# Splitting the expert combine of an MoE layer into two F32R passes with one-hot rows, and moving the token gather between two transposes

## The chip, the cores and the metric

One core of a Trainium2 chip (trn2) runs the whole program. The metric is the device time of one execution in microseconds (us). Timings of such a program differ a little from run to run, so times are medians of several runs, and changes are judged beside runs of the unchanged kernel.

## What is computed

One layer of a hybrid encoder on 256 tokens of 1024 features, all float32: a mixer (differential attention on half of the channels, a gated linear recurrence on the other half), a LayerNorm, then a mixture of experts (top 4 of 32), and a last LayerNorm. Only the mixture is touched here. Cut to what matters:

```python
def clamped_swiglu(h):
    x_glu = jnp.minimum(h[..., ::2], 7.0)
    x_lin = jnp.clip(h[..., 1::2], -7.0, 7.0)
    return x_glu * jax.nn.sigmoid(1.702 * x_glu) * (x_lin + 1.0)

def moe(x, w_router, b_router, w_gu, b_gu, w_down, b_down):
    logits = xt @ w_router + b_router
    top_v, top_e = lax.top_k(logits, 4)
    gates = jax.nn.softmax(top_v, axis=-1)
    ...
    def expert_block(args):
        tok, g, e = args
        xb = xt[tok]
        h = xb @ w_gu[e] + b_gu[e]
        y = clamped_swiglu(h) @ w_down[e] + b_down[e]
        return y * g[:, None].astype(y.dtype)
    ...
    out = jax.ops.segment_sum(ys.reshape(R, D), row_tok, num_segments=T)
```

Each expert has 12 MB of float32 weights (8 MB in `w_gu`, 4 MB in `w_down`), so that the 32 experts read some 403 MB from HBM.

## The kernel before

After the mixer and the router, the program walks over the 32 experts (`for e in range(NE - 1)`, line 1090, and a tail for the last one from line 1126). Each expert has 64 slots (CAP) for its tokens; slots beyond that are computed in an overflow path behind a branch (`overflow`, `more`), which this input takes once. The work of expert e, in the order in which TensorE (PE) does it:

1. `first(e)`: the up projection (`gu_mm`, L892), 64 matmuls into the PSUM tiles h0 and h1. The four 2 MB chunks of `w_gu` are used one after the other. Behind each half VectorE (DVE) and ScalarE (ACT) compute the clamped SwiGLU (`swiglu`, L902 to L906); for the second half this begins when the last matmul is through.
2. `finish(e % 2)`: the combine (L954) of the pair of experts before: the output rows of two experts lie on 128 partitions, and a matmul with the transposed gate matrix `gt` (slots by tokens, the gate's value where slot and token meet, else 0) spreads them over the tokens. DVE adds the result to `acc` (L956). One half of the tokens is combined in the even expert behind the pair, the other half in the odd one.
3. In an even expert GpSimd (POOL) builds the gate rows `sgate` for the pair (`gate_rows`, L940). In an odd one PE transposes them (`gate_t`, L948) and ACT copies them out of PSUM as `gt` (L950).
4. For each half b: two transposes of the activations (`act_t`, L913) into PSUM, ACT copies them out (L914), and `begin_gu` starts the PSUM tile h of the next expert with its bias (L679).
5. `need(...)`: a matmul with a one-hot matrix S gathers one half of the next pair's token rows (`gather_mm`, L797); ACT (even) or DVE (odd) copies them out (L807, L805). POOL makes S (L784).
6. The down projection (`down_mm`, L925), 32 matmuls into the tiles y0 and y1, and, after an odd expert, ACT copies both to SBUF (L1117) for the combine.

Steps 2 to 5 stand between the up and the down projection of one expert. The transposes, the gather, the combine and the copied gates all take their PSUM tiles from one pool of three buffers (`mc`), so that each of them waits until the reader of an earlier tile is done. The order on PE and on the DMA queue (SP) is the program's; on DVE, ACT and POOL a scheduler sets it when the program is built, except in the tail, where DVE and ACT are ordered by hand.

The weights come over SP's queue in the order of use (`load_chunk`), into ten buffers of 2 MB (`SLOTS`): each load waits until PE is through with the chunk that lay in its buffer.

In the tail, expert 31 and the last LayerNorm: four PSUM tiles `fps` collect `acc` and the last combines (`fin`, L1130). Two of these matmuls are strewn between the down projection of expert 30 (`todo`), and four follow the last down projection, after ACT and DVE have copied y0 and y1 (L1166, L1167).

## Time and profile before

| | |
|---|---|
| median of 3 runs | 1098.46 us (1097.53 to 1099.27) |
| the profiled execution | 1100.57 us, its span 1098.9 us |
| granted TensorE clock, mean | 0.979 of full speed |
| PE busy | 1008.3 us (92%) |
| DVE, ACT, POOL busy | 277.8, 188.7, 146.6 us |
| read from HBM | 420.52 MB, 384 GB/s over the span |

The span is what lies between the first and the last instruction that the profiler saw; the execution's time has some 1.7 us more around it. [...] The durations of matmuls are those of one instruction from start to end; since they are pipelined, the distance from start to start is what they cost.

### The profile page before, as it was taken

The page shows a single profiled execution, that of the slowest core. Times are in us where ns is not written, and L with a number is a line of the kernel's source. Part 1 is how long each engine was busy: PE and PEld are TensorE (multiplying, and loading weights), DVE is VectorE, ACT ScalarE, POOL GpSimd, SP SyncE. Part 2 cuts the span into 40 slices and gives each one's busy share as a digit, 9 for nine tenths or more (in the row PEclk, how much of TensorE's full clock was granted, in tenths as well). Part 3 has the DMA queues.
Part 4 walks back from the last instruction along what each step waited for, and adds up shares of the span by engine and source line. Part 5 has one row for each costly group of instructions (what it writes and reads, how often), then busy time and mean ns, then how long its engine had stood idle before and what let it go on. Part 6 is the DMA issues. An engine that isn't in the chain of part 4 may idle for free. (4 is left out here: it accounts for less than half of the span.)

```text
span 1098.9 us, 12603 instructions
## 1 busy us (share of the span) xinstructions
PE 1008.3 (92%) x4948; PEld 472.8 (43%) x4948; DVE 277.8 (25%) x625; ACT 188.7 (17%) x426; POOL 146.6 (13%) x221
## 2 busy tenths in 40 slices
PE   8999999999999889888999989888888989999995
PEld 8987644443444333333334433333323434444431
DVE  6978411121212121213212121212101222121223
ACT  5576211111111111110011111110100101111111
POOL 4583202010101010101001010101001001010101
PEclk8999999999999999999899999999999989999998
DMA  7967799999999999999999999999999949999972
GB/s 268 334 247 318 293 377 426 422 423 423 423 423 423 422 423 423 422 425 426 423 424 420 410 423 412 420 410 394 415 395 411 423 198 424 425 425 422 424 292 82
DMA packets 47193, 423.44 MB, mean 385 GB/s; under 512 B 6365, under 2 KB 6430, under 8 KB 14400
## 3 DMA queue, kind: packets, MB, share of 16 engines
q1 hardware_dynamic: 47040, 421.59, 92.9%
q8 instruction: 73, 1.20, 0.5%
q14 instruction: 80, 0.66, 0.2%
HBM read 420.52 MB, written 1.05 MB: 384 GB/s over the span
## 5 line engine op out<-in xcount | busy, mean ns | idle before, releaser
L892 PE MATMUL h<-we,xg 128*64 128x512 f32 (+1 forms) x2112 | 469.8, 603 | 63.1 <-DMA we<-in_w_gu_dram 50.6
L892 PEld LDWEIGHTS h<-we,xg 128*64 128x64 f32 (+1 forms) x2112 | 161.9, 137 | 368.3 <-issue 295.1
L925 PE MATMUL y<-we,actT 128*64 128x512 f32 x1024 | 228.9, 599 | 0.1
L902 DVE TENSOR_SCALAR g<-h 128x256 f32<-128x256 f32 x65 | 27.6, 425 | 688.3 <-PE h L892 688.3
L940 POOL TENSOR_SCALAR sgate<-iota,posm,gate 128x64 f32<-128x64 f32 x96 | 54.1, 582 | 814.2 <-PE gt_ps L948 813.2
L925 PEld LDWEIGHTS y<-we,actT 128*64 128x64 f32 x1024 | 71.3, 137 | 135.1 <-issue 127.7
L903 ACT ACTIVATE sg<-g 128x256 f32<-128x256 f32 x65 | 27.0, 416 | 589.2 <-DVE g L902 589.2
L797 PE MATMUL xg_ps<-S,n 128*128 128x128 f32 (+1 forms) x544 | 70.5, 284 | 0.0
L797 PEld LDWEIGHTS xg_ps<-S,n 128*128 128x128 f32 x544 | 69.5, 199 | 2.5 <-issue 1.6
L954 PE MATMUL cb<-ysb,gtT 128*128 128x512 f32 x116 | 57.5, 618 | 0.0
L1117 ACT ACTIVATE ysb<-y 128x512 f32<-128x512 f32 x30 | 16.3, 594 | 140.7 <-PE y L925 140.7
L956 DVE TENSOR_TENSOR acc<-acc,cb 128x512 f32<-128x512 f32 x58 | 39.5, 680 | 0.0
L805 DVE TENSOR_SCALAR xg<-xg_ps,gb 128x128 f32<-128x128 f32 (+1 forms) x68 | 22.8, 398 | 61.8 <-PE xg_ps L797 61.8
L389 PE MATMUL pj<-xh,hi 128*128 128x256 f32 x128 | 37.3, 292 | 0.0
L389 PE MATMUL pj<-xh,lo 128*128 128x256 f32 x128 | 36.8, 288 | 0.0
L389 PE MATMUL pj<-xo,hi 128*128 128x256 f32 x128 | 36.8, 288 | 0.0
L913 PE MATMUL actT_ps<-ident,g 128*128 128x128 f32 x130 | 29.9, 312 | 7.3 <-DVE g L906 6.3
L954 PEld LDWEIGHTS cb<-ysb,gtT 128*128 128x128 f32 x116 | 19.6, 189 | 37.4 <-ACT sg L903 23.5
L252 POOL TENSOR_TENSOR lo<-win,hi 128x1024 fp32r<-128x1024 f32 x11 | 32.9, 3014 | 12.3 <-PE pj L389 12.2
L913 PEld LDWEIGHTS actT_ps<-ident,g 128*128 128x128 f32 x130 | 21.6, 202 | 24.8 <-DVE g L906 12.2
L807 ACT ACTIVATE xg<-xg_ps,gb 128x128 f32<-128x128 f32 (+1 forms) x68 | 25.4, 452 | 33.2 <-PE xg_ps L797 33.2
L679 PE MATMUL h<-bgu,pick 128*128 128x512 f32 x64 | 30.5, 479 | 0.0
(271 smaller groups left out, 702.5 us busy)
## 6 DMA issues: line engine op xcount, KB each, us to landing
we<-in_w_gu_dram SPq DMA_DIRECT2D x128, 2048.0 KB, 15.3
we<-in_w_down_dram SPq DMA_DIRECT2D x127, 1024.0 KB, 30.4
win<-in_w_in_dram SPq DMA_DIRECT2D x8, 1024.0 KB, 9.8
wout<-in_w_out_dram SPq DMA_DIRECT2D x4, 1024.0 KB
win<-in_w_in_dram SPq DMA_DIRECT2D x4, 512.0 KB, 8.2
x<-in_x_dram SPq DMA_DIRECT2D x4, 256.0 KB, 3.1
we<-in_w_down_dram SPq DMA_DIRECT2D x2, 512.0 KB
out_dram<-acc SPq DMA_DIRECT2D x4, 256.0 KB, 2.3
```

The lines of the kernel that those rows point to most:

```text
L252: return (eng or V).tensor_sub(lo, src, f32(hi))
L389: PE.matmul(ps[m // 2][:, m % 2], a, b, start=k == 0 and m % 2 == 0 and i == 0, stop=k == KT - 1 and i == 2, skip_group_check=True)
L679: PE.matmul(ps[b], picks[e].rearrange("p g w -> p (g w)"), bgs[b], start=True, stop=False, skip_group_check=True)
L797: PE.matmul(ps[:, (k % 4) * n:(k % 4 + 1) * n], pairs(n1[t])[:, k // 2, k % 2], S[:, t], start=start, stop=t == NT - 1, skip_group_check=True)
L892: PE.matmul(ps[b][g * w:(g + 1) * w], xg[k // 4][:, k % 4, o:o + w], W[e, k][:, c0:c0 + 512], start=False, stop=k == KT - 1, skip_group_ch ...
L902: V.tensor_scalar(g[:, ns], ps[b][:, 0::2], 7.0, None, op0=OP.min)
L903: A.activation(s, g[:, ns], AF.Sigmoid, scale=1.702)
L913: PE.transpose(ps[:, j * P:(j + 1) * P], gj[:, j], ident)
L925: PE.matmul(ps[n][gs], at[:, 2 * b + j, g * CAP:(g + 1) * CAP], w_dn(e, 2 * g + b, j, n * 512, 512), start=c + j == 0, stop=c + j == 4, sk ...
L940: G.tensor_scalar(sg[:, t, i * CAP:(i + 1) * CAP], iota2[:, 0], posm[:, t, o:o + 1], gate[:, t, o:o + 1], op0=OP.is_equal, op1=OP.mult)
L954: PE.matmul(pp, gt[:, n, t * P:(t + 1) * P], y, start=True, stop=True)
L956: V.tensor_add(acc[t][:, ns], acc[t][:, ns], pp)
```

## The change

The gates leave the combine's matrix. `gate_t` still transposes the gate rows, but ACT now copies them with two instructions, one for each expert of the pair's slot block, each of which also sums its rows (`accum_out`): since a slot holds one token, the sum is the slot's gate, in a column `gs`. POOL then turns the copy `gg` into a matrix of zeros and ones (`is_gt`), typed float32r. `weighted` takes the place of the two plain copies of y: ACT writes the gated rows as a float32r high part, and DVE (`scalar_tensor_tensor`) what is left of them as a low part. The combine is then two F32R matmuls, high and low, in place of one float32 matmul, both in the loop and in `fin`. In the tail, too, ACT and DVE now write a high and a low part of both tiles. Apart from that the gather (`need`) moves from behind both halves' transposes to between them.

```diff
-    def ytile(e, n):
-        return wk.tile([P, 512], F32, tag=f"y{n}", bufs=1, name=f"ysb{e}_{n}")
+    def weighted(e, n, src, gs):
+        hi, lo = [wk.tile([P, 512], F32R, tag=f"y{i}{n}", bufs=1, name=f"y{i}_{e}_{n}") for i in range(2)]
+        A.activation(hi, src, AF.Copy, scale=gs[:, n:n + 1])
+        V.scalar_tensor_tensor(lo, src, gs[:, n:n + 1], f32(hi), op0=OP.mult, op1=OP.subtract)
+        return hi, lo
 
     def gate_rows(e):
...
                 PE.transpose(ps[:, n, t * P:(t + 1) * P], sg[:, t, n * CAP:n * CAP + P], ident)
-        gt = wk.tile([P, 2, T], F32, tag="gtT", bufs=1, name=f"gtT{e}")
-        A.activation(gt, ps, AF.Copy)
-        return gt
+        gs = wk.tile([P, 2], F32, tag="gs", name=f"gs{e}")
+        gg = wk.tile([P, 2, T], F32, tag="ggT", bufs=1, name=f"ggT{e}")
+        for n in range(2):
+            A.activation(gg[:, n], ps[:, n], AF.Identity, bias=zero_t, accum_out=gs[:, n:n + 1])
+        gt = wk.tile([P, 2, T], F32R, tag="gtT", bufs=1, name=f"gtT{e}")
+        G.tensor_scalar(gt, gg, 0.0, None, op0=OP.is_gt)
+        return gt, gs
 
     def combine(t, n, y, gt, pp):
-        PE.matmul(pp, gt[:, n, t * P:(t + 1) * P], y, start=True, stop=True)
+        for i in range(2):
+            PE.matmul(pp, gt[:, n, t * P:(t + 1) * P], y[i], start=i == 0, stop=i == 1)
...
             if e < NE - 2:
                 begin_gu(e + 1, (b,))
-        need(where[e][0] + 1, G, where[e][1])
+            if b == 0:
+                need(where[e][0] + 1, G, where[e][1])
...
         if e % 2:
-            pend = [ytile(e, n) for n in range(2)], gt
-            for n in range(2):
-                A.activation(pend[0][n], ps[n], AF.Copy)
+            pend = [weighted(e, n, ps[n], gs) for n in range(2)], gt
...
         A.activation(warm, eps_t, AF.Sqrt)
-        A.activation(y[0], ps[0], AF.Copy)
-        V.tensor_copy(y[1], ps[1])
+        y = [weighted(e, n, ps[n], gs) for n in range(2)]
         for t in range(NT):
             fin(t, gt, y, stop=True)
```

What the change moves is read from the order of the instructions as built (the line numbers of the changed kernel are up to ten higher; [waits ...] names the engines whose results an instruction waits for). First PE in expert 29, an odd one, between its up and its down projection; cb are the combine's tiles, gt_ps the transposed gates, actT_ps the transposed activations, h30 the next expert's bias, xg_ps the gather. Before:

```order
L954 MATMUL cb29_0_33999<-ysb27_0_31894,gtT27_31843 128x512 [waits DVE_49,PE_49,Activation_49]
L954 MATMUL cb29_1_34002<-ysb27_1_31895,gtT27_31843 128x512 [waits DVE_49]
L948 MATMUL gt_ps29_34005<-ident_169,sgate28_32921 128x128 x4
L913 MATMUL actT_ps29_34013<-ident_169,g29_33984 128x128 [waits DVE_49]
L679 MATMUL h30_0_34019<-bgu0_148,pick30_34017 128x512
L913 MATMUL actT_ps29_34021<-ident_169,g29_33984 128x128 [waits DVE_49]
L679 MATMUL h30_1_34025<-bgu1_149,pick30_34017 128x512 [waits PE_49]
L797 MATMUL xg_ps_34028<-S30_32943,n1_0_1213 128x128 [waits Activation_49]
```

And with the change:

```order
L964 MATMUL cb29_0_34165<-y0_27_0_32054,gtT27_32003 128x512 [waits DVE_49,PE_49,Activation_49]
L964 MATMUL cb29_0_34165<-y1_27_0_32055,gtT27_32003 128x512
L964 MATMUL cb29_1_34169<-y0_27_1_32058,gtT27_32003 128x512 [waits DVE_49]
L964 MATMUL cb29_1_34169<-y1_27_1_32059,gtT27_32003 128x512
L952 MATMUL gt_ps29_34173<-ident_169,sgate28_33087 128x128 x4
L913 MATMUL actT_ps29_34185<-ident_169,g29_34150 128x128 [waits DVE_49]
L679 MATMUL h30_0_34191<-bgu0_148,pick30_34189 128x512
L797 MATMUL xg_ps_34194<-S30_33103,n1_0_1213 128x128 [waits PE_49,Activation_49]
L913 MATMUL actT_ps29_34207<-ident_169,g29_34150 128x128 [waits DVE_49]
L679 MATMUL h30_1_34211<-bgu1_149,pick30_34189 128x512
```

The gather now stands ahead of the second half's transposes, and its PSUM tile is the one that gt_ps held: it waits for ACT to have read the gates out. Next ACT in the same expert, before:

```order
L903 ACTIVATE sg29_33986<-g29_33984 128x256
L903 ACTIVATE sg29_33993<-g29_33984 128x256
L950 ACTIVATE gtT29_34010<-gt_ps29_34005 128x512
L914 ACTIVATE actT29_34012<-actT_ps29_34013 128x256
L914 ACTIVATE actT29_34012<-actT_ps29_34021 128x256
```

And with the change:

```order
L903 ACTIVATE sg29_34152<-g29_34150 128x256
L903 ACTIVATE sg29_34159<-g29_34150 128x256
L957 ACTIVATE ggT29_34179,gs29_34178<-gt_ps29_34173,zero_t_177 128x256 x2
L914 ACTIVATE actT29_34184<-actT_ps29_34185 128x256
L914 ACTIVATE actT29_34184<-actT_ps29_34207 128x256
```

One copy has become two that also sum, at the same place. Last DVE between the two projections of expert 28, from the second half's SwiGLU on, before:

```order
L902 TENSOR_SCALAR g28_32900<-h28_1_31858 128x256 [waits PE_49]
L904 TENSOR_SCALAR l28_32908<-h28_1_31858 128x256
L905 SCALAR_TENSOR_TENSOR l28_32908<-l28_32908,g28_32900 128x256 [waits DVE_49]
L956 TENSOR_TENSOR acc0_78<-acc0_78,cb28_0_32915 128x512 [waits PE_49]
L906 TENSOR_TENSOR g28_32900<-l28_32908,sg28_32909 128x256 [waits DVE_49,Activation_49]
L956 TENSOR_TENSOR acc0_78<-acc0_78,cb28_1_32918 128x512 [waits PE_49]
```

And with the change:

```order
L902 TENSOR_SCALAR g28_33064<-h28_1_32032 128x256 [waits PE_49]
L904 TENSOR_SCALAR l28_33072<-h28_1_32032 128x256
L966 TENSOR_TENSOR acc0_78<-acc0_78,cb28_0_33079 128x512 [waits PE_49]
L905 SCALAR_TENSOR_TENSOR l28_33072<-l28_33072,g28_33064 128x256 [waits DVE_49]
L966 TENSOR_TENSOR acc0_78<-acc0_78,cb28_1_33083 128x512 [waits PE_49]
L906 TENSOR_TENSOR g28_33064<-l28_33072,sg28_33073 128x256 [waits DVE_49,Activation_49]
```

Both additions to acc now stand ahead of the last step of the SwiGLU (L906), where one stood before. The odd experts and expert 30 have the same order. SP's queue holds the same loads in the same order.

## Rows read from the trace of the kernel before

**Rows 1.** Waits between engines, whole span: who waited, us in all, times, longest.

```profile
PE h L892 <- DMA we<-in_w_gu_dram: 50.6, 39, 2.4
```

**Rows 2.** Windows: length, busy us of PE, PEld, DVE, ACT, POOL (instructions), clock, DMA share, GB/s.

```profile
720.00:760.00 40.00, 32.79 (x152) 12.45 (x154) 4.95 (x12) 3.44 (x10) 0.00 (x0) 1.00 0.98 398
...
896.00:900.00 4.00, 3.56 (x11) 0.99 (x10) 0.76 (x2) 0.00 (x0) 0.00 (x0) 0.59 0.08 29
...
1062.00:1064.00 2.00, 2.00 (x12) 0.61 (x10) 1.82 (x5) 0.42 (x1) 0.00 (x0) 1.00 0.42 172
```

**Rows 3.** Timeline of PE, 850 to 1099 us: start, length, instruction, idle before it.

```profile
879.85 3.50 PE L892 MATMUL h<-we,xg 128*32 128x512 f32 x16 [2.40 <-DMA we<-in_w_gu_dram]
...
896.83 15.58 PE L892 MATMUL h<-we,xg 128*64 128x512 f32 x64 [0.45 <-PEq L1017]
```

**Rows 4.** SP's own waits, 860 to 930 us.

```profile
SPq L199 <- PE h L892: 25.9, 3, 19.9
```

**Rows 5.** PE by line, 897 to 1085 us: busy us, mean ns, idle before.

```profile
L892 PE MATMUL h<-we,xg 128*64 128x512 f32 x448 | 99.7, 602 | 1.3 <-PEq L1011 0.9 <-PEq L1017 0.4
```

**Rows 6.** Timeline, 962 to 980 us: expert 27 (odd) between its projections.

```profile
964.94 1.98 PE L954 MATMUL cb<-ysb,gtT 128*128 128x512 f32 x4
...
965.39 0.41 DVE L904 TENSOR_SCALAR l<-h 128x256 f32<-128x256 f32 x1
...
966.18 0.68 DVE L956 TENSOR_TENSOR acc<-acc,cb 128x512 f32<-128x512 f32 x1
...
966.76 0.60 PE L948 MATMUL gt_ps<-ident,sgate 128*128 128x128 f32 x4
...
966.77 0.42 DVE L906 TENSOR_TENSOR g<-l,sg 128x256 f32<-128x256 f32 x1
...
967.39 0.60 ACT L950 ACTIVATE gtT<-gt_ps 128x512 f32<-128x512 f32 x1 [1.42 <-PE gt_ps L948]
...
968.42 2.04 PE L797 MATMUL xg_ps<-S,n 128*128 128x128 f32 x16
...
970.39 7.09 PE L925 MATMUL y<-we,actT 128*64 128x512 f32 x32
```

**Rows 7.** Timeline, 988 to 1000 us: expert 28 (even).

```profile
991.55 1.98 PE L954 MATMUL cb<-ysb,gtT 128*128 128x512 f32 x4
...
996.40 4.08 PE L925 MATMUL y<-we,actT 128*64 128x512 f32 x18
```

**Rows 8.** Timeline of PE, 84 to 128 us: F32R matmuls of 512 columns behind float32 transposes.

```profile
113.49 0.48 PE L653 MATMUL mix<-hio,rech 128*128 128x512 f32 x1
113.81 0.40 PE L653 MATMUL mix<-hio,reco 128*128 128x512 f32 x1
114.05 0.40 PE L653 MATMUL mix<-loo,rech 128*128 128x512 f32 x1
```

**Rows 9.** Timeline of ACT, 53 to 62 us: copies of 256 columns that also sum.

```profile
56.06 0.49 ACT L453 ACTIVATE s<-s,mx 128x256 f32<-128x256 f32 x1
...
56.55 0.49 ACT L453 ACTIVATE s<-s,mx 128x256 f32<-128x256 f32 x1
56.95 0.19 ACT L453 ACTIVATION_READ_ACCUMULATOR s<-s,mx 128x1 f32 x1
```

**Rows 10.** Timeline, 1040 to 1099 us: experts 30 and 31 and the tail.

```profile
1045.97 0.42 DVE L906 TENSOR_TENSOR g<-l,sg 128x256 f32<-128x256 f32 x1
...
1066.32 0.60 PE L948 MATMUL gt_ps<-ident,sgate 128*128 128x128 f32 x4
...
1067.63 0.51 PE L913 MATMUL actT_ps<-ident,g 128*128 128x128 f32 x2 [0.47 <-ACT actT L914]
...
1072.85 1.12 PE L1130 MATMUL fin<-ysb,gtT 128*128 128x512 f32 x2
...
1084.14 0.60 ACT L1166 ACTIVATE ysb<-y 128x512 f32<-128x512 f32 x1 [6.60 <-PE y L925]
...
1088.53 0.70 DVE L1173 BATCH_NORM_STATS2 st<-fin 128x6 f32<-128x512 f32 x1
```

## The prediction

> **What bounds the kernel now.** First the waits between engines: PE waited 39 times for weights at the up projection, 50.6 us in all, so that the weights' transfers set the pace somewhere [rows 1]. Then windows, to see where. From 160 us to 880 us the transfers are at work all the time; from 720 us to 760 us, for one, with a share of 0.98, while PE is busy for only 32.79 of 40 us [rows 2]. There a faster PE only waits longer. Then PE's timeline around the one overflow, in front of expert 25. PE still waits 2.40 us for weights in it, at 879.85 us [rows 3]; whatever PE won or lost before is forgotten there. While the overflow runs, all ten buffers fill up, and SP waits 19.9 us for PE to free the next one [rows 4]: the transfers are then half an expert behind, but PE has ten chunks in hand. Expert 25 begins at 896.83 us [rows 3], and from there to the last down projection the up projections idle for 1.3 us in all, none of it for weights [rows 5]. The transfers are at work all that time too, but PE is behind them: their share falls in the window that begins at 1062 us, when the last chunk lands [rows 2], and PE needs that chunk in the second half of the down projection that ends at 1084.14 us [rows 10], in the last 3.5 us or so. That leaves PE a good 15 us to win before the weights could bind again.

> So the change counts for what it does to PE from 896.83 us on, in experts 25 to 31, and in the tail. The 23 combines before that are worth nothing, and what the changed gates cost there costs nothing, because the wait at 879.85 us takes both up.

> **The combine itself.** The four instructions of one expert's combine take 1.82 us to the next instruction's start (964.94 to 966.76 us [rows 6]). Four F32R matmuls of the same shape: behind float32 work the first takes 0.32 us to the next start, the following ones 0.24 us [rows 8], so about 1.02 us. PE saves 0.80 us per expert, if nothing else is late.

> [...]

> **Even experts (26, 28).** The first half's transposes follow at 1.02 us, the bias at about 1.17 us, the gather at about 1.5 us: it needs the tile of the first combine, which DVE has read by then (below). The gather takes 1.97 us to the next start [rows 6], and now covers the second half's SwiGLU, which ends at about 2.75 us. With 0.5 us for the second transposes and bias the down projection begins at 4.0 us. It began at 4.85 us (991.55 to 996.40 us [rows 7]). Saving: 0.85 us each, 1.7 us for both.

> **DVE's new order.** In expert 27 the second half's L904 begins 0.45 us behind the combine's start, an addition takes 0.59 us to the next start, and the last step, L906, begins at 1.83 us [rows 6]. Now the first addition begins at 0.80 us (L904 takes 0.35 us) and ends near 1.48 us; L905, with 0.34 us, and the second addition, with 0.59 us, follow, and L906 begins at about 2.32 us, 0.49 us later than before, and ends at 2.75 us. Where the gather stands in between this is hidden. Its cover is gone in expert 30, which has no gather: there the second half's transposes wait for L906, which ran at 1045.97 us [rows 10] and comes 0.49 us later. Cost: 0.5 us, once.

> **Odd experts (25, 27, 29).** The transposed gates now begin at 1.02 us, and ACT can read them 0.63 us later (966.76 to 967.39 us [rows 6]), at 1.65 us. It now runs two copies of 256 columns that sum. Such copies start 0.49 us apart, and the read of the sum ends 0.59 us behind the second's start [rows 9]: 1.08 us, or 2.7 us on this clock. The gather needs this very tile and waits for the second sum, some 1.2 us behind its place in the line; it began at 3.48 us and now at about 2.75 us. Then 1.97 us of gather and 0.5 us of transposes and bias: the down projection begins at 5.2 us. It began at 5.45 us [rows 6]. Saving: 0.2 us each, 0.6 us for three. Those copies read SBUF and also take an exponential; the nearest other row is the plain copy of 512 columns out of PSUM, 0.60 us [rows 6]. If the two sums together take no longer than that, 0.7 us are saved; if each takes as long, nothing is. These are the bounds; I stay with the row that sums.

> **Expert 31 and the tail.** The two sums stand in front of the activations on ACT here as well. They could begin at 1066.95 us and end at 1068.0 us, and the second transposes, which ran at 1067.63 us [rows 10], now wait for them: 0.4 us lost (0 to 0.9 us; the upper end is both sums and one more copy). The two combines strewn between the down projections take 1.06 us each (1072.85 us to the next down matmul); as F32R 0.32 + 0.24 us and the same 0.1 us of changeover: 0.4 us saved each, 0.8 us. Behind the last down projection ACT writes the first high part in 0.60 us from 1084.14 us, DVE the low part in 0.7 us behind it, then the second; the last matmuls are no longer four slow ones in a row. DVE, with two low parts and four statistics to do one behind the other, is the limit: its last statistics ran at 1088.53 us [rows 10] and come at about 1088.3 us. I take 0.2 us; the bounds are 0.5 us lost, if each high part holds up its low part and the matmul behind it, and 0.5 us saved.

> **Costs put at nothing.** DVE's low parts and POOL's `is_gt` run behind the down projections, 14 us or more ahead of the combine that reads them; POOL is busy for 146.6 of 1098.9 us. On POOL the next S stands behind `is_gt`, and the gather that reads it comes 20 us later. No load moves on SP. The low parts free y0 and y1 about a microsecond later; the next pair needs these some 20 us later.

> **The sum**: 1.7 + 0.6 - 0.5 - 0.4 + 0.8 + 0.2 = 2.4 us saved. Against the profiled execution's 1100.57 us that is 1098.2 us; that execution is 2.1 us above the median of the runs, and the span's proportions hold for both, so against 1098.46 us I predict **1096.1 us**. With all bounds at their worst the saving is about 0.6 us, at their best 4.6 us: 1093.9 to 1097.9 us.

> **Rivals.**
> - *The new waits don't bind.* If ACT's sums and DVE's additions are ahead of PE, each of the six combines saves its 0.80 us, or 0.85 us, and the tail 1.0 us: 5.9 us, 1092.6 us. For it: the gather as a cover is long. Against it: its PSUM tile is the gates' own, and the row for ACT's start leaves little doubt.
> - *The waits eat the saving.* If each sum on ACT takes 0.2 us longer than the row says and the tail's splits cost 0.5 us, the odd experts lose 0.2 us each and some 0.5 us remain: 1098.0 us, no change. For it: two engines, ACT and DVE, now work in series where each had one copy.
> - *The clock falls* (the slower side). In each odd expert PE now stands still for about 1.2 us in front of the gather, behind low work. If the granted clock falls on that, the next up projection pays: behind the overflow, with 0.59 granted in its first 4 us [rows 2], one took 15.58 us [rows 3], where the others average 14.0 us ((99.7 - 15.58) / 384 x 64 [rows 5]). Three times 1.6 us are 4.8 us, less 2.4 us: 1100.9 us. It decides if the clock falls in two of the three. Against it: from 720 to 760 us PE stood still for 7.2 us in pieces and the granted clock was 1.00 [rows 2]. [...]

> **How the numbers follow.** The sum 0.68, waits not binding 0.10, waits eating the saving 0.17, the clock 0.05. A measurement of this kernel can tell about 0.2% from no change, 2.2 us, and the sum lies just beyond that: 0.43 of its 0.68 go to faster and 0.25 to the same. Faster is 0.43 + 0.10 = 0.53, slower 0.05 and 0.01 from the second rival, the same 0.25 + 0.16 = 0.41. The range takes the sum's bounds, most of the second rival, and 0.7 us above it for the spread of the runs; it leaves the first rival and the third out: 1093.8 to 1098.6 us.

> **What would show it.** In the profile after: combines of four F32R instructions in about 1.0 us; even experts with 4.0 us and odd ones with 5.2 us from combine to down projection; in odd ones the gather waiting for ACT; the wait at about 879.85 us and the start of expert 25 where they were; no wait for weights behind it. It would be wrong if expert 25 began elsewhere by more than a microsecond, or if PE waited for weights again behind it.

## The result, and the profile after

The changed kernel takes 1105.17 us (median of 5 runs, 1103.85 to 1105.42), the kernel before 1098.46 us beside it (5 runs): a ratio of 1.0055, 95% interval 1.0040 to 1.0069. By that ratio it is slower by 6.0 us (4.4 to 7.6 us), and the prediction had it faster. The profiled execution of the changed kernel is its median run, with a span of 1103.4 us, 4.5 us more than before's, whose profiled execution was 2.1 us above its median.

The steps that the prediction named did what it said, nearly. An odd expert between its projections, in the timeline of the changed kernel (start, length, engine and line, instruction, idle before):

```profile
970.35 1.20 PE L964 MATMUL cb<-y,gtT 128*128 128x512 f32 x4
...
971.39 0.60 PE L952 MATMUL gt_ps<-ident,sgate 128*128 128x128 f32 x4
...
972.09 0.47 ACT L957 ACTIVATE ggT<-gt_ps,zero_t 128x256 f32<-128x256 f32 x1 [0.69 <-PE gt_ps L952]
...
972.66 0.42 DVE L906 TENSOR_TENSOR g<-l,sg 128x256 f32<-128x256 f32 x1
972.91 0.20 ACT L957 ACTIVATION_READ_ACCUMULATOR ggT<-gt_ps,zero_t 128x1 f32 x1
...
973.16 2.15 PE L797 MATMUL xg_ps<-S,n 128*128 128x128 f32 x16 [0.56 <-ACT ggT L957]
...
975.70 4.51 PE L925 MATMUL y<-we,actT 128*64 128x512 f32 x20
```

The four F32R matmuls take 1.04 us to the next start, where the old combine, two float32 matmuls that the profile shows as four instructions, took 1.82 us [rows 6]. ACT's two sums take 1.02 us (972.09 to 973.11 us), the gather waits for the second, and the down projection begins 5.35 us behind the combine; it was 5.45 us [rows 6]. An even expert, from the same view:

```profile
996.86 1.20 PE L964 MATMUL cb<-y,gtT 128*128 128x512 f32 x4
997.89 0.39 PE L913 MATMUL actT_ps<-ident,g 128*128 128x128 f32 x2
...
998.46 1.77 PE L797 MATMUL xg_ps<-S,n 128*128 128x128 f32 x13
```

Its down projection begins at 1000.98 us, 4.12 us behind the combine; it was 4.85 us [rows 7].

What nobody had asked for stands in the waits between engines from 897 us on (who waited for what: us in all, times, longest):

```profile
PE h L892 <- issue: 3.1, 1, 3.1
PE xg_ps L797 <- ACT ggT L957: 1.6, 3, 0.6
PE actT_ps L913 <- DVE g L906: 1.4, 1, 1.4
PE actT_ps L913 <- ACT ggT L957: 0.9, 1, 0.9
PE fin L1143 <- ACT y L934: 0.9, 1, 0.9
PE h L892 <- PEq L1021: 0.9, 5, 0.2
```

"issue" is time in which PE waited for nothing that the profile shows. Before, the up projections stood for 1.3 us in this stretch, all of it PEq, PE's sequencer [rows 5]. PE's timeline has the place, the up projection of expert 26:

```profile
897.61 15.65 PE L892 MATMUL h<-we,xg 128*64 128x512 f32 x64 [0.45 <-PEq L1027]
...
925.82 2.33 PE L892 MATMUL h<-we,xg 128*64 128x512 f32 x9 [0.19 <-PEq L1021]
931.23 13.93 PE L892 MATMUL h<-we,xg 128*64 128x512 f32 x55 [3.09 <-issue]
945.09 1.21 PE L964 MATMUL cb<-y,gtT 128*128 128x512 f32 x4
```

After some ten matmuls (9 in this trace) PE stands for 3.09 us. From the start of this up projection to its combine are 19.27 us; the next experts take 13.88 us. The windows show the rest of the loss (length, busy us of PE, PEld, DVE, ACT, POOL, granted clock, DMA share, GB/s):

```profile
928.00:932.00 4.00, 0.91 (x4) 0.19 (x2) 0.00 (x0) 0.00 (x0) 0.00 (x0) 1.00 1.04 428
932.00:936.00 4.00, 4.00 (x13) 1.27 (x14) 0.00 (x0) 0.00 (x0) 0.00 (x0) 0.57 0.78 272
936.00:940.00 4.00, 4.00 (x22) 1.50 (x20) 0.00 (x0) 0.00 (x0) 0.00 (x0) 1.00 0.95 342
```

In the 4 us behind the stop 0.57 of the clock is granted (in windows of 1 us from 932 us on 0.52, 0.50, 0.50 and 0.77), and the 55 matmuls that are left take 13.86 us to the combine, where 55/64 of 13.88 us are 11.9 us. So the stop costs 5.39 us in all: some 3.5 us of standing, from start to start, and 1.9 us of clock.

No gap in the transfers goes with it: their share is 1.04 while PE stands. But among them are instructions. In the 16 us around the stop the table of DMA queues (queue, kind: packets, MB, share) has three such packets:

```profile
q8 instruction: 3, 0.05, 1.2%
```

Over the whole span it has 72 with 1.18 MB in the changed kernel, some 16 KB each: code comes in pieces while the kernel runs, beside the weights. The middle one of the three runs from 928.73 to 929.75 us: it begins 0.6 us behind PE's stop, and PE goes on 1.5 us behind its end.

That queue 8 carries PE's code is read from such times. In the traces of the kernel before and the changed one PE stands six times for more than 1 us for "issue" in an up projection (1.56 to 2.59 us before, 2.69 to 3.69 us after), and each time it goes on 1.3 to 2.3 us behind the end of a packet of this queue.

The account in the two traces: expert 25 begins at 897.61 us in place of 896.83 us [rows 3], +0.8 us; from there to the end are 205.79 us in place of 202.07 us, +3.7 us: 5.4 us for the stop, less 1.7 us that the change saves.

### The profile page after: what moved, and what is told of

It is laid out like the page before. It is cut to its first block, busy times and chain, and to the rows that moved or that the text cites. A ratio compares the mean times of both kernels' runs of the same rounds, so it can differ in the third digit from the quotient of the medians.

```text
span 1103.4 us, 12801 instructions
## 1 busy us (share of the span) xinstructions
PE 993.1 (90%) x4948; PEld 468.9 (42%) x4948; DVE 300.1 (27%) x656; ACT 197.0 (18%) x475; POOL 173.4 (16%) x237
## 3 DMA queue, kind: packets, MB, share of 16 engines
q8 instruction: 72, 1.18, 0.4%
## 5 line engine op out<-in xcount | busy, mean ns | idle before, releaser
L892 PE MATMUL h<-we,xg 128*64 128x512 f32 (+1 forms) x2112 | 479.9, 614 | 74.3 <-DMA we<-in_w_gu_dram 58.5
L944 POOL TENSOR_SCALAR sgate<-iota,posm,gate 128x64 f32<-128x64 f32 x96 | 57.4, 613 | 794.8 <-PE gt_ps L952 793.9
L797 PE MATMUL xg_ps<-S,n 128*128 128x128 f32 (+1 forms) x544 | 73.6, 290 | 7.1 <-ACT ggT L957 7.1
L935 DVE SCALAR_TENSOR_TENSOR y<-y,gs,y 128x512 fp32r<-128x512 f32 x32 | 22.6, 746 | 122.9 <-ACT y L934 122.9
L934 ACT ACTIVATE y<-y,gs 128x512 fp32r<-128x512 f32 x32 | 20.3, 684 | 127.9 <-PE y L925 127.9
L964 PE MATMUL cb<-y,gtT 128*128 128x512 f32 x116 | 34.7, 421 | 0.0
L913 PE MATMUL actT_ps<-ident,g 128*128 128x128 f32 x130 | 27.5, 293 | 6.9 <-DVE g L906 5.6
L959 POOL TENSOR_SCALAR gtT<-ggT 128x512 fp32r<-128x512 f32 x16 | 23.8, 1490 | 52.8 <-PEq L1021 52.8
L914 ACT ACTIVATE actT<-actT_ps 128x256 f32<-128x256 f32 x64 | 24.7, 386 | 40.8 <-PE actT_ps L913 40.8
```

The costliest lines, as they stand in the source:

```text
L797: PE.matmul(ps[:, (k % 4) * n:(k % 4 + 1) * n], pairs(n1[t])[:, k // 2, k % 2], S[:, t], start=start, stop=t == NT - 1, skip_group_check=True)
L892: PE.matmul(ps[b][g * w:(g + 1) * w], xg[k // 4][:, k % 4, o:o + w], W[e, k][:, c0:c0 + 512], start=False, stop=k == KT - 1, skip_group_ch ...
L913: PE.transpose(ps[:, j * P:(j + 1) * P], gj[:, j], ident)
L944: G.tensor_scalar(sg[:, t, i * CAP:(i + 1) * CAP], iota2[:, 0], posm[:, t, o:o + 1], gate[:, t, o:o + 1], op0=OP.is_equal, op1=OP.mult)
L964: PE.matmul(pp, gt[:, n, t * P:(t + 1) * P], y[i], start=i == 0, stop=i == 1)
```

## The experiments

**The theory.** PE's code arrives late at one place. In front of each expert PE jumps over the overflow block, some 2,280 instructions where an expert runs about 260, and goes on where it lands. I counted PE's instructions in the programs as built (labels left out), supposing that its code is cut into equal pieces, one to a packet of some 16 KB. How many instructions a packet holds is my assumption: no run shows it. By it the "issue" stops of the two traces, in experts 5, 15 and 24 before and 5, 16 and 26 after, lie in experts where a piece ends at much the same distance behind the landing. Two experts of the changed kernel where it does so too show none: 6, and 25, which ran its overflow block; so this place alone does not make a stop. The change adds one or two instructions to an expert (a run of 257 and 262 in place of 255 and 261), and these add up until another expert has the unlucky place. In experts 5 to 24 PE waits for weights sooner or later anyway (39 waits before, 50.6 us in all [rows 1]), so by this theory a stop costs nothing there; expert 26 is bound by PE. **Rivals:** the loss comes from the changed steps themselves, or a chunk of weights came late behind the overflow.

**Code that is moved and never run.** Transposes are added in expert 0's overflow block, which this input jumps over. What is executed stays the same; all of PE's code behind it moves by two instructions for each.

```diff
             PE.transpose(ps[:, t * P:(t + 1) * P], sg[:, t], ident)
+        if e == 0 and i == 1:
+            for _ in range(113):
+                PE.transpose(ps[:, P:2 * P], sg[:, 1], ident)
```

> The changed kernel; 113 more transposes stand in expert 0's overflow block, which this input jumps over: nothing more is executed, but all PE code behind it lies 226 instructions further on. Theory (PE's code arrives late in expert 26, where PE is the bound): by the count of PE's instructions from each branch's landing, the stop of 3.09 us moves from expert 26 to expert 24, where PE waits for weights anyway. Expert 26's up projection takes 13.9 us again instead of 19.3 us, and the time falls by about 5.4 us to 1099.8 us (1098.5 to 1101). Rival 1 (the loss comes from the changed steps: gates, gather, two-pass combine): no change, 1105 us. Rival 2 (a late weight chunk behind the overflow): no change either, the weights' queue is the same.

> The changed kernel with 36 such transposes (72 instructions). Theory of late code: the stop moves from expert 26 to expert 28, which is also bound by PE; expert 26's up projection 13.9 us, expert 28's about 19 us, the time as the changed kernel's, 1105 us (1103.5 to 1106.5). Rival 2 (a late weight chunk): the stop stays in expert 26.

> The kernel before, with 41 such transposes (82 instructions). Theory of late code: its stop moves from expert 24, where it costs nothing, to expert 27: up projection there about 19 us instead of 13.9 us, the time 1098.5 + 5.4 = 1103.9 us (1102 to 1105). Rivals 1 and 2: no change, 1098.5 us, since neither the changed steps nor a weight chunk is touched.

> The kernel before, with 113 such transposes (226 instructions): a control, by the theory the stop goes to expert 23, where PE waits for weights anyway, so no change: 1098.5 us (1097.3 to 1100). If more code alone cost something, it would show here as it would in the changed kernel with the same 113.

Measured, all beside the same runs of the kernel before (1099.54 us), with what the trace has from the start of expert 25 to the end (before 202.07 us, changed 205.79 us):

| kernel | median us | ratio, 95% interval | from expert 25 on, us |
|---|---|---|---|
| changed, 113 transposes | 1097.83 | 0.9976 (0.9962 to 0.9991) | 200.42 |
| changed, 36 | 1106.08 | 1.0053 (1.0039 to 1.0068) | 207.52 |
| before, 41 | 1103.06 | 1.0042 (1.0025 to 1.0060) | 205.43 |
| before, 113 | 1099.88 | 1.0007 (0.9991 to 1.0024) | 202.06 |

With 113 transposes the changed kernel has no stop behind the overflow, and is faster than the kernel before: 2.0 us below the 1099.8 us that I expected, and below the range given with it (a second measurement below has 1098.03 us). The stop was expected in expert 24; the trace has stops in experts 4 and 15 alone. PE's timeline of it, and its instruction packets in the 16 us around the same place:

```profile
919.76 3.60 PE L925 MATMUL y<-we,actT 128*64 128x512 f32 x16
923.55 11.81 PE L892 MATMUL h<-we,xg 128*64 128x512 f32 x54 [0.19 <-PEq L1024]
```

```profile
q8 instruction: 2, 0.03, 0.8%
```

The up projection runs through, 13.88 us to its combine at 937.43 us, and one packet less was fetched in that window. With 36 transposes the stop leaves expert 26, but comes in expert 29, not in expert 28 as I had counted: the count is good to one expert. Its timeline shows it, with a wait of 1.95 us at the landing (0.16 to 0.19 us elsewhere); with that the trace is 7.1 us longer than the one with 113 transposes:

```profile
1004.26 2.80 PE L892 MATMUL h<-we,xg 128*64 128x512 f32 x12 [1.95 <-PEq L1024]
1010.64 12.95 PE L892 MATMUL h<-we,xg 128*64 128x512 f32 x52 [3.58 <-issue]
```

And in the kernel before, with not one of its steps changed, the stop can be put into expert 27 (its timeline, and a window from there):

```profile
949.67 2.80 PE L892 MATMUL h<-we,xg 128*64 128x512 f32 x12 [0.16 <-PEq L1014]
955.60 11.38 PE L892 MATMUL h<-we,xg 128*64 128x512 f32 x52 [3.13 <-issue]
```

```profile
956.00:960.00 4.00, 4.00 (x22) 1.42 (x20) 0.00 (x0) 0.00 (x0) 0.00 (x0) 1.00 1.01 426
```

Here the clock stays at 1.00 behind the stop, and the up projection takes 17.24 us, 3.36 us more, where I had expected 5.4 us more. The control is unchanged. Both rivals fall: within each pair, the changed kernel with and without the transposes and the kernel before with and without them, neither the steps that run nor the weights' queue differ.

**The parts alone, and the instruction that announces the branch.** In the first three kernels PE's code is placed so that its last stop lies in front of expert 25.

x5, from the changed kernel, puts the gather back behind both transposes:

```diff
-            if b == 0:
-                need(where[e][0] + 1, G, where[e][1])
+        need(where[e][0] + 1, G, where[e][1])
```

> The changed kernel with the gather back behind both halves' transposes, so that the two-pass combine stands alone; PE's code placed as in the changed kernel with 113 transposes (stop in front of expert 25). Theory (the parts need each other): the second half's transposes wait for L906, which now runs behind both additions, about 2.8 us behind the combine's start, and the gather follows it uncovered: 5.3 us from combine to down projection in even experts (before 4.85) and in odd ones (before 5.45). Two even experts lose 0.45 us each, expert 30 0.5 us, three odd ones win 0.15 us each, the tail 0.4 us: about 0.5 us slower than the kernel before, a ratio near 1.0005. Rival (the combine's own 0.8 us counts whatever stands behind it): 2.4 us and more faster, 0.9976, like the whole change with its code so placed.

x6, from the kernel before, puts it between them and changes nothing else:

```diff
-        need(where[e][0] + 1, G, where[e][1])
+            if b == 0:
+                need(where[e][0] + 1, G, where[e][1])
```

> The kernel before with the gather between the transposes alone, one-pass combine and gates as before, PE's code placed likewise. Theory: even experts stay at 4.85 us from combine to down projection, since the slow combine had covered the second half's SwiGLU already; odd ones wait for the one copy of the gates and stay near 5.5 us: no change, ratio 1.000 (0.999 to 1.001). Rival (the gather's new place is what helps): 1.5 us faster, 0.9986.

x7, from the changed kernel, copies the gates once and sums them on DVE:

```diff
-        for n in range(2):
-            A.activation(gg[:, n], ps[:, n], AF.Identity, bias=zero_t, accum_out=gs[:, n:n + 1])
+        A.activation(gg, ps, AF.Copy)
+        V.tensor_reduce(gs, gg, axis=AX.X, op=OP.add)
```

> The changed kernel with one copy of the gates on ACT (512 columns, 0.60 us) in place of two that sum, and the sums by one reduction on DVE behind L906; PE's code placed likewise. Theory: in odd experts the gather waits for ACT's second sum, about 0.5 us beyond the one copy; without it the gather begins near 2.3 us behind the combine in place of 2.8 us. Three odd experts and expert 31 win 0.5 us each, 2 us: ratio near 0.9958, 1.9 us below the changed kernel so placed. Rival (another wait stands right behind the sums, DVE's additions or the transposes' copy): as the changed kernel so placed, 0.9976.

x8, from the changed kernel with its code where it was, announces the next branch later:

```diff
-        g = first(e, lambda i: (i == 3 and ready(e + 1), e == 0 and i == 6 and need(0, V, 1)))
+        g = first(e, lambda i: (i == 10 and ready(e + 1), e == 0 and i == 6 and need(0, V, 1)))
```

> The changed kernel, its code where it was, but PE's instruction that announces the next branch (and the load of the count ahead of it) stands behind 40 matmuls of the up projection instead of 12. If the stop belongs to that instruction, expert 26's up projection stops near its 40th matmul, about 8.7 us in, or not at all; if it belongs to a fixed place in PE's code, it stops after 10 to 12 matmuls as before, and the time stays 1105 us.

| kernel | median us (before 1099.21) | ratio, 95% interval | from expert 25 on, us |
|---|---|---|---|
| x5, combine alone | 1100.42 | 1.0010 (1.0001 to 1.0019) | 203.03 |
| x6, gather alone | 1098.95 | 0.9991 (0.9974 to 1.0008) | 201.81 |
| x7, sums on DVE | 1097.70 | 0.9985 (0.9976 to 0.9994) | 197.00 |
| x8, announced later | 1105.72 | 1.0052 (1.0037 to 1.0068) | 205.74 |

The combine alone does not help, it costs 1 us. In its timeline, expert 28, the second transposes wait for L906, which now stands behind both additions:

```profile
994.22 1.20 PE L964 MATMUL cb<-y,gtT 128*128 128x512 f32 x4
...
997.00 0.50 PE L913 MATMUL actT_ps<-ident,g 128*128 128x128 f32 x2 [1.12 <-DVE g L906]
...
999.55 1.94 PE L925 MATMUL y<-we,actT 128*64 128x512 f32 x8
```

5.33 us, where the kernel before took 4.85 us: a faster matmul in front of the same steps of DVE, in their new order, became a wait. The gather alone gives 0.15 us in each even expert (4.71 us) and nothing in the odd ones. Only together do they save: the gather then covers the SwiGLU that the old combine had covered.

With the sums on DVE the wait behind ACT's second sum goes (expert 27):

```profile
963.21 1.19 PE L964 MATMUL cb<-y,gtT 128*128 128x512 f32 x4
...
965.58 2.15 PE L797 MATMUL xg_ps<-S,n 128*128 128x128 f32 x16
...
968.12 2.37 PE L925 MATMUL y<-we,actT 128*64 128x512 f32 x10
```

4.91 us in place of 5.34 us in odd experts, and 0.5 us in the tail, as expected. Of its 197.00 us, 1.5 us are not its doing: expert 25's up projection took 13.98 us here, near the 13.88 us of expert 26's at a granted clock of 1.00, and 15.4 to 15.6 us in every other trace. The median shows no gain: the ratio was expected near 0.9958 and is 0.9985, beside 0.9976 with the sums on ACT.

In x8 the announcement stands 28 matmuls later, and PE still stops in expert 26 after the same ten matmuls, for 2.99 us. So the stop does not belong to that instruction; it stays at its place in the code.

**A version with both, and repeats.** In expert 30 no gather covers the wait for L906 (1.36 us). There the combine is put behind the second half's transposes, on top of x7:

```diff
-        finish(e % 2)
+        if e < NE - 2:
+            finish(e % 2)
...
+            if b == 1 and e == NE - 2:
+                finish(e % 2)
```

> The changed kernel with the gates' sums on DVE and, in expert 30 alone, the combine behind the second half's transposes, so that L906 runs ahead of both additions there; PE's code placed with the stop in front of expert 25. Theory: expert 30 takes about 3.2 us from the second half's end to expert 31's up projection in place of 3.7 us; with the sums the stretch from expert 25's combine on is 2.2 us shorter than the changed kernel's, ratio 0.996 to 0.998 to the kernel before. Rival (the clock around the overflow covers such sizes): no difference to the two below that can be measured.

> The changed kernel with the gates' sums on DVE, code placed likewise, once more beside the other two: ratio 0.9976 to 0.9994 as before, 0.5 us above the version with expert 30's combine moved.

> The changed kernel with 113 transposes in expert 0's overflow block, once more: ratio 0.9962 to 0.9991 as before; if the gates' sums on DVE are worth what the trace shows in their stretch, 1 to 2 us above the version with the sums on DVE.

| kernel | median us (before 1099.16) | ratio, 95% interval | from expert 25 on, us |
|---|---|---|---|
| x9, sums on DVE and expert 30 | 1097.65 | 0.9983 (0.9973 to 0.9993) | 198.69 |
| x10, sums on DVE | 1098.52 | 1.0000 (0.9985 to 1.0015) | 199.54 |
| x11, changed, 113 transposes | 1098.03 | 0.9988 (0.9977 to 0.9999) | 200.21 |

The intervals overlap: the runs do not tell the three apart, and x11, expected 1 to 2 us above x10, lies 0.5 us below it. Expert 30's new order gained nothing. Its timeline has the transposes still waiting for L906, with the combine now uncovered behind them:

```profile
1042.92 0.51 PE L913 MATMUL actT_ps<-ident,g 128*128 128x128 f32 x2 [1.24 <-DVE g L906]
1043.18 1.18 PE L964 MATMUL cb<-y,gtT 128*128 128x512 f32 x4
...
1044.75 7.52 PE L892 MATMUL h<-we,xg 128*64 128x512 f32 x34
```

From expert 30's up projection to expert 31's are 17.71 us, in x10 17.58 us. What x10 lost against x9 is another thing, in expert 31's up projection of x10:

```profile
1042.97 7.09 PE L892 MATMUL h<-we,xg 128*64 128x512 f32 x32
1050.94 1.94 PE L892 MATMUL h<-we,xg 128*64 128x512 f32 x8 [0.88 <-DMA we<-in_w_gu_dram]
```

PE is now early enough to wait for weights again. That takes back part of what the sums on DVE save. From expert 25's start PE needs 147.8 us to this up projection in x10, 150.5 us in the kernel before. The limit lies at one time of the span: the chunk that x10 waits for, the third of expert 31, lands there at 1050.89 us. In x1, x7, x9 and x11 it lands at 1050.4 to 1050.9 us, and PE comes to it 0.4 to 0.8 us later, so that they do not wait. With the code well placed hardly a microsecond is left to win on PE here; in the kernel before it was 3.5 us (landed at 1050.78 us, used from 1054.26 us).

With its code well placed the change is faster than the kernel before in both measurements, by 2.6 and 1.3 us (x1, x11). I know no version that is measurably better than that. x1, x9 and x11 beat both kernels, the change as it was made by some 7 us; the version with the sums on DVE was faster than the kernel before once (x7) and even with it once (x10).

## Why the prediction was wrong

- **What bounds the kernel** held in the changed kernel: no wait for weights behind the overflow, and PE's stops in front of it cost nothing. But "a good 15 us to win before the weights could bind again" was far too much: it looked at the last chunk alone. x10 waits for an earlier one, in expert 31's up projection, with 2.7 us won since expert 25's start, and in the kernel before PE came to that chunk 3.5 us behind its landing.
- **The step that failed** is "Costs put at nothing", and before it the 1.3 us of idle time [rows 5] taken over to the changed kernel. PE's stream was costed by what it executes. That it also has a length, that code comes while the kernel runs (72 packets of some 16 KB on queue 8), and that the edit moves its place, stood in no term. The trace of before had the sign: four waits of PE for "issue", 6.4 us in all, the longest 2.6 us, in experts 5, 15 and 24. By the prediction's own reading of what bounds those experts they cost nothing there, and so I read past them; what they were and what would move them was the question to ask. The term is 5.4 us, from one place in expert 26. None of the signs that the prediction named as speaking against it came (expert 25's start moved by less than 1 us, and no wait for weights stood behind it): none of them looked at PE's code.
- **Even experts**: 0.85 us each predicted, 0.73 and 0.74 us measured. **The combine**: 1.02 us predicted, 1.04 us measured.
- **Odd experts**: 0.2 us each predicted, 0.10 to 0.12 us measured; the wait for the second sum is there, and x7 shows that it is worth 0.43 us.
- **Expert 30**: 0.5 us lost predicted, 0.49 us measured (3.20 to 3.69 us). **Expert 31 and the tail**: 0.6 us saved predicted, about 0.4 us measured.
- **The sum** from expert 25 on, without the stop: 2.4 us predicted, 1.65 and 1.86 us in the two traces with the code moved, 2.6 and 1.3 us by the runs. Sign and place were right for the steps that the sum had, and the traces have 0.69 and 0.78 of its size.
- **The clock rival** was right that PE standing can cost clock and wrong on where: PE's 0.56 us in front of the gather left the next up projections at 13.88 us. The stop in expert 26 did cost clock: 0.57 was granted in the 4 us behind it.
- **Expert 25's start** came 0.8 us later. In the eleven traces of the experiments it lies between 894.1 and 900.4 us; whether the change has a part in the 0.8 us stays open.

## What to carry to other kernels

A wait for "issue" in the middle of a run of equal matmuls was a cost that moves: 36 transposes that never run took it from expert 26 to expert 29, and 41 put one into expert 27 of the kernel before. So ask where the code for it came from, and whether an edit that adds a few instructions per loop pass put it there. Before judging a change of a few microseconds, run it once with its code moved by instructions that are never executed, and the kernel before likewise; here two placements of the same kernel lay 8.3 us apart (1097.83 and 1106.08 us), several times what the change itself is worth. And a faster step in front of a chain on another engine saved only what the next step in line could cover: the combine and the gather were worth nothing apart (ratios of 1.0010 and 0.9991), and 0.9976 and 0.9988 together.

## What the runs showed of the hardware

A stop of 3.1 us was followed by 0.57 of the clock for 4 us in one kernel (changed, expert 26) and by full clock in another (before with 41 transposes, expert 27), so its price was 5.4 us or 3.4 us. What decides between the two is not shown.
